# Two-layer hybrid decoder kernel: where the sums of the output weights' quarters are made, the order of the seven products, and which norms fold their halves

## The chip, the cores and the metric

The kernel runs on 1 core of one Trainium2 chip. The metric is device time in microseconds; times are given as the median of 3 runs. A difference of about 0.2% (2.67 us) is what a measurement of this kernel can tell from none.

## The reference, cut to what matters

Two layers act on x of 512 tokens by 1024 channels, float32. Each layer normalises x, multiplies by one wide input matrix, runs differential attention (8 heads) and an mLSTM in chunked form (8 heads), gates both, projects each, merges them to u, and adds an output projection:

```python
for l in range(DEPTH):
    h = rmsnorm(x, norm_g)
    proj = h @ w_in
    ...
    oa = rmsnorm(oa, attn_norm_g) * (1.0 - lam_init)
    ya = (oa * silu(az)) @ w_out_a
    hb = rmsnorm(hb, mlstm_norm_g)
    yb = (sigmoid(bo) * hb * silu(bz)) @ w_out_b
    u = sigmoid(ga) * ya + sigmoid(gb) * yb
    x = x + u @ w_o
```

## The kernel before, in words

Every product is made in three matmuls of high and low parts (`mm3`, L493): an operand a is split into a rounded high part and the rest (`split`, L489: ScalarE copies, VectorE subtracts), and the product takes high times high, high times low and low times high. A weight piece is 128 x 1024 numbers, 512 KB. It is loaded by SyncE into a tile `wr` (tag `raw`, two buffers), split into `wh` and `wl` (three buffers each), and used by TensorE for 24 matmuls of 512 columns, or, for a piece of the output projection, 12.

The output projection `u @ w_o` ("wo") is made in seven half-size products instead of eight (Strassen-Winograd, `seven`, L763). Each product P1 to P7 has two pieces (halves a = 0 and 1) of 12 matmuls. The chains X, Y and Z are accumulators of two banks each (L760): P1, P6, P7 and P4 add up in X, P5 and P3 in Y, P2 in Z. P1, P2 and P3 take quarters of the weights as they are; P5, P6, P7 and P4 take sums of quarters: T1 = first + second quarter, T2 = T1 + a third, T3 = two quarters, T4 = T2 + the last. Before the change these sums are made in SBUF, in tiles `ws_wo` and `wt_wo` out of a pool of 20 slots (`add_up`, L1465): SyncE loads the first quarter into the tile, and a GpSimd DMA that accumulates adds the next. T1 and T3 are made some 12 pieces ahead (`acl`). T2 takes T1's place in the same tile, so its adding transfer can start only when P5's piece has been split out of it, and T4's only after P6's (`prep`, L1505). The order of products is P1 P5 P3 P6 P2 P7 P4, so that P3 covers the time of T2's transfers.

The output's upper right quarter is residual minus X minus Y; in the order before, both are read after P6 (`post`, L767; `wo_out`, L1002).

A sum over the 128 channels of a head, for the norms and the mLSTM's denominator, is a matmul with ones (`psum_over`, L1267). Plain, the squares are split into two tiles and take two matmuls (`hi_lo`, L1262). Folded (`fold`, L1252), the lower 64 partitions' squares get those of the upper 64 added, high and low halves share one tile, and one matmul does; ScalarE makes the square in two instructions of 64 partitions, and VectorE has one more addition. `foldA` lists the attention heads that fold, `foldM` the mLSTM heads for the norm, `foldD` those for the denominator.

The order of work on every engine comes from a planner (`Recorder.schedule`, L272) that records all instructions, gives each a due time worked back from TensorE's order, and takes at each step the ready one with the least due time. Links from a tile's last reader to the next user of its buffer count in the due times (`soft`, L292). SyncE takes what is ready in order of recording. `TUNE` holds the order of the pieces, the due-time margins (`bias` shifts them by tile name) and the offsets of the heads' steps.

Of the kernel before, what the change touches and what calls it, by code (L numbers as in the profile page):

```python
# [18 lines left out]
P = 128  # L19
# [16 lines left out]

TUNE = {
    "order": (
# [4 lines left out]
    ),  # L43
    "qkt": 5,
    "gct": 15,
    "gls": 6,
    "glf": 5,
    "attn": (1, 5, 5, 8, 9, 13, 15, 16, 19, 24),
    "a0": 23,
    "ap": 18,  # L50
    "a4": 7,
    "ml": (1, 9, 11, 12, 13, 28),
    "ahead": 3,
    "lc": 7,
    "slack": 4956.0,
    "margin": 72.0,
    "pemargin": 171.8,
    "wait": 333.1,
    "swpen": 701284048.1,
    "smargin": 51.6,  # L60
    "pwait": 0.8,
    "wdiff": 3673.3,
    "wsp": 4,
    "kact": (0, 2),
    "qsq": (1, 3),
    "foldA": (2, 3, 5),
    "foldM": (0, 1, 2, 3, 4, 7),
    "foldD": (0, 1, 2, 3, 4, 5, 6, 7),
    "warm": 18,
    "start": 'x0 ct ng w0 x1 w1 x2 x3',  # L70
    "prods": 'P1 P5 P3 P6 P2 P7 P4',
    "acl": 12,
    "gateA": 9,
    "gateM": 0,
    "actp": (0, 2, 3),
    "m0": 218,
    "mp": 15,
    "m4": 11,
    "slots": 20,
    "bias": {'av': 27450.0, 'msp_a': -4350.0, 'wl': 2400.0, 'wo': -3700.0, 'woh': -4650.0, 'ht': 29150.0, 'taz': -4050.0, 'ga': 16050.0, 'gt': -8800.0, 'p': -300.0, 'wo1_P': 23900.0, 'out_0_dram': -5900.0, 'p5_wo': -4950.0, 'rot': 12650.0, 'dq': -4400.0, 'oa': 450.0, 'dd': 30900.0, 'num': 20100.0, 'ld': -4700.0, 'ws1_wo': -1200.0, 'gw': -1100.0, 'hl': -350.0, 'sc': -1400.0, 'uz': -3750.0, 'mk': 7250.0, 'sbz': 550.0, 'az': 10300.0, 'posi': -650.0, 'msl_d': 1650.0, 's1_wo': 1700.0, 'wob': 50.0, 'msh_d': 6450.0, 'sq': -1600.0, 'warm': 3150.0, 'bo': -400.0, 'sdl': 200.0, 'ml': 15800.0, 'fo_b': 11200.0, 'ws0_wo': -900.0, 'wt1_wo': 1300.0, 'pb': 2000.0, 'sbo': 5350.0, 'qkt': 2000.0, 'junk': 6150.0, 'ulZ': 7650.0, 'bv': 650.0, 'bqk': -1750.0, 'uh': -3950.0, 'ms_b': -1550.0, 'gi': 1000.0, 'ob': 250.0, 'uy': 1750.0, 'gcol': -750.0, 'ms': 11250.0, 'cosv': -4100.0, 'ms_a': 1450.0, 'ones': 2450.0, 'msh_b': 6650.0, 'x1d': -1650.0, 'qt': 1100.0, 'qk0_2x': -6300.0, 'fb_a': 4650.0, 'saz': 900.0, 'xr': -2300.0, 'fb_b': 900.0, 'wo0_P': 450.0, 'qk1_0x': 1950.0, 'fb_d': -5800.0, 'msh_a': 2700.0, 'ulA': -150.0, 'ang': 150.0, 'rnh': 1400.0, 'gft': 6600.0, 'gct': 200.0, 'gc': -300.0, 'mql': -1200.0, 'rows': 150.0, 'kl': -700.0, 'posf': -150.0, 'zw': 2400.0, 'qk1_2x': -3000.0, 'gf': 450.0, 'qk0_0x': -50.0, 'uhY': 7150.0, 'qs': 3050.0, 'qy': 250.0, 'ul': -500.0, 'msl_a': 2800.0, 'uhZ': 7800.0, 'lneps': -950.0, 'gm': -4350.0, 'lq': 450.0, 'x': -3700.0, 'eps': -700.0, 'sgb': 150.0, 'wr': -400.0, 'wt0_wo': -300.0, 'stab': 8000.0, 'xn': 1200.0, 'qss': 150.0, 'den': 2000.0, 'msl_b': 950.0, 'rn': -150.0, 'glf': 900.0, 'ss': 4250.0, 'bz': -100.0, 'sdh': -200.0, 'em': -250.0, 'uhB': 850.0, 'rq': 250.0, 'sinv': -1650.0},  # L80
    "drain": 251.9,
    "risk": 295.5,
    "late": 912.7,
}


# [358 lines left out]
def kernel(ctx, tc, x, pos, wp, wg, cst, par, pb, ngb, out):  # L445
# [162 lines left out]
    def give(n):  # L608
        state["q2"] -= n
# [16 lines left out]
    def layer_events(l):  # L626
# [136 lines left out]
        def seven(name, lhs, out, over):  # L763
# [63 lines left out]
        def qk_done(c, tt, acc):  # L827
# [38 lines left out]
            st[("rot", tt % 2)] = rq  # L866
            if tt % 2 == 0:
# [592 lines left out]
    def source(l, n, kh, c, a):  # L1460
        return wp[l, KIDX[n, c, 2 * kh + a]]

    chains = {}

    def add_up(l, n, t, a):  # L1465

        if t == "T1":
            take(1)
            chains[n, a] = q2w(f"ws{l}_{n}_{a}", F32)
            SY.dma_start(chains[n, a], source(l, n, 0, 0, a))  # L1470
            G.dma_start(chains[n, a], source(l, n, 0, 1, a), accum_op=ALU.add)
        elif t == "T3":
            take(1)
            chains[n, a, 3] = q2w(f"wt{l}_{n}_{a}", F32)
            SY.dma_start(chains[n, a, 3], source(l, n, 0, 1, a))
            G.dma_start(chains[n, a, 3], source(l, n, 1, 1, a), accum_op=ALU.add)
        else:
            G.dma_start(chains[n, a], source(l, n, 1, 1 if t == "T2" else 0, a), accum_op=ALU.add)

    def load(i):  # L1480
        if i >= len(pieces) or i in loaded:
            return
        l, key = pieces[i]
        if key[0] == "seven":
            _, n, prod, a = key
            if prod in ("P1", "P2", "P3"):
                w = wpool.tile([P, 1024], F32, tag="raw", bufs=2, name=f"wr{i}")
                SY.dma_start(w, source(l, n, *{"P1": (0, 0), "P2": (1, 0), "P3": (1, 1)}[prod], a))
                loaded[i] = w
            return  # L1490
# [7 lines left out]
    def load_sums(i):  # L1498

        if i < len(pieces) and pieces[i][1][0] == "seven" and pieces[i][1][2] in ("P5", "P7") and ("sum", i) not in loaded:  # L1500
            l, (_, n, prod, a) = pieces[i]
            add_up(l, n, {"P5": "T1", "P7": "T3"}[prod], a)
            loaded["sum", i] = True

    def prep(i):  # L1505
        if i >= len(pieces) or i in ready:
# [8 lines left out]
            return  # L1515
        wh = wpool.tile([P, 1024], F32R, tag="wh", name=f"wh{i}")
        wl = wpool.tile([P, 1024], F32R, tag="wl", name=f"wl{i}")
        if key[0] == "seven" and key[2] in ("P5", "P6", "P7", "P4"):
            _, n, prod, a = key
            load_sums(i)  # L1520
            t = chains[n, a, 3] if prod == "P7" else chains[n, a]
            split(wh, wl, t)
            if prod in ("P5", "P6"):
                add_up(l, n, "T2" if prod == "P5" else "T4", a)
            else:
                give(1)
        elif i < TUNE["wsp"]:
            A.copy(wh, loaded[i])
            for hf in range(2):
                cs = slice(S * hf, S * hf + S)  # L1530
                V.tensor_tensor(wl[:, cs], loaded[i][:, cs], wh[:, cs].bitcast(F32), ALU.subtract)
        else:
            split(wh, wl, loaded[i])
# [8 lines left out]
            SY.dma_start(ng0 if n == "ng" else ct, ngb[0] if n == "ng" else cst)  # L1542
    late_loads()
    prep(0)
    for i, run in enumerate(runs):
        if i in starts:
            starts[i](state["t"])
        for a in range(3):
            load(i + a)
        for a in range(TUNE["acl"] + 1):  # L1550
            load_sums(i + a)
        for a in range(TUNE["ahead"]):
            prep(i + a)
        for _ in run(*ready[i]):
# [86 lines left out]
```

## Time and profile before

| | |
|---|---|
| median of 3 runs | 1334.37 us (1334.32 to 1335.81) |
| the profiled execution's own time | 1334.56 us |
| its span, first to last instruction | 1332.5 us |
| TensorE busy | 1325.0 us, 6200 matmuls |
| VectorE busy | 1018.0 us, 1846 instructions |
| ScalarE busy | 907.8 us, 1836 instructions |
| GpSimd busy | 36.9 us, 44 instructions |
| DMA | 148.14 MB, mean 111 GB/s |
| granted TensorE clock | 1.000 |

Busy time is the union of an engine's instructions. Matmuls overlap in the records: one of 512 columns is recorded at some 390 ns, while the next starts earlier, so what a matmul costs is read from a run of them, start to end. `PEld` is the loading of the stationary operand, which overlaps. Lines named `q` (SPq) are a queue's issuing instructions. L441 is the one line from which the planner issues everything, so rows are told apart by tile names.

### The profile page before, as it was taken

Reading aid. Unit: us, or ns where it says so; the run is one execution under the profiler, and the core shown is the slowest. Engines: PE = TensorE matmul, PEld = TensorE weight load, DVE = VectorE, ACT = ScalarE, POOL = GpSimd, SP = SyncE. Lnnn points to the kernel's source line nnn. Section 1 sums busy time; section 2 is a strip of 40 time slices with the busy share of each in tenths; the row PEclk is TensorE's granted clock in tenths of the full one; section 3 lists DMA queues with packets and bytes.
Section 4 is the critical chain, followed back from the end, with each engine's and each line's share of the span. In section 5 each row is a group of like instructions: output and inputs, shape, how many; then the busy total and the mean of one; then the engine's idle time right before and its main releaser. Section 6 shows DMA issues by size and latency. Waiting matters only on the chain.

```text
span 1332.5 us, 17532 instructions
## 1 busy us (share of the span) xinstructions
PE 1325.0 (99%) x6200; PEld 1095.0 (82%) x6200; DVE 1018.0 (76%) x1846; ACT 907.8 (68%) x1836; POOL 36.9 (3%) x44
## 2 busy tenths in 40 slices
PE   9999999999999999999999999999999999999998
PEld 7888888888888888888788888888888888888886
DVE  7898899786259968755888988997852699687566
ACT  6878798877247858743667787889762489687343
POOL 1000000000000000000200000000000000000000
PEclk9999999999999999999999999999999999999999
DMA  5222222223333443554833122222332344354646
GB/s 188 87 67 78 80 83 64 91 79 99 95 103 112 149 123 113 146 155 128 248 112 95 49 95 64 79 76 83 82 112 79 128 119 141 99 135 135 170 122 182
DMA packets 51272, 148.14 MB, mean 111 GB/s; under 512 B 6096, under 2 KB 12880, under 8 KB 51184
## 3 DMA queue, kind: packets, MB, share of 16 engines
q1 hardware_dynamic: 48880, 138.63, 32.9%
q0 software_dynamic: 2304, 8.39, 3.6%
q8 instruction: 49, 0.80, 0.2%
q14 instruction: 39, 0.32, 0.1%
HBM read 142.74 MB, written 4.26 MB: 110 GB/s over the span
## 4 chain that ended last, share of the span: by engine, by line
PE 98%; ACT 1%; DMA 0%; SPq 0%; DVE 0%; issue 0%; DVEq 0%
PE qk L441 13%; PE av L441 9%; PE az L441 7%; PE bv L441 7%; PE bqk L441 7%; PE bz L441 7%; PE bo L441 7%; PE gb L441 7%; PE ga L441 7%; PE woa L441 7%; PE wob L441 7%; PE wo_P L441 6%; PE sc L441 3%; PE num L441 2%; PE ms L441 1%; PE ut L441 1%
## 5 line engine op out<-in xcount | busy, mean ns | idle before, releaser
L441 ACT CAST wh<-wr 128x1024 fp32r<-128x1024 f32 (+1 forms) x206 | 214.8, 1045 | 190.0 <-PE ga L441 36.3
L441 DVE TENSOR_TENSOR wl<-wr,wh 128x1024 fp32r<-128x1024 f32 (+1 forms) x208 | 248.9, 1200 | 99.7 <-ACT wh L441 98.9
L441 PE MATMUL qk<-wh,hh 128*128 128x512 f32 x256 | 96.1, 401 | 0.5 <-ACT hh L441 0.5
L441 PE MATMUL qk<-wh,hl 128*128 128x512 f32 x256 | 95.3, 400 | 0.1
L441 PE MATMUL qk<-wl,hh 128*128 128x512 f32 x256 | 94.8, 396 | 0.5 <-DVE wl L441 0.5
L441 ACT ACTIVATE p<-sc,mx,rq 128x128 f32<-128x128 f32 (+3 forms) x128 | 78.8, 618 | 16.2 <-DVE mx L441 15.6
L441 PE MATMUL woa<-oa,wh 128*128 128x512 f32 x256 | 87.8, 390 | 0.0
L440 ACT ACT_TABLE_LOAD x65 | 83.4, 1283 | 1.1
L441 PE MATMUL wob<-ob,wh 128*128 128x512 f32 x256 | 83.4, 389 | 0.0
L441 PEld LDWEIGHTS qk<-wl,hh 128*128 128x128 f32 x256 | 48.0, 188 | 10.2 <-DVE wl L441 0.9
L441 PEld LDWEIGHTS wob<-ob,wh 128*128 128x128 f32 x256 | 48.1, 188 | 10.1
L441 PEld LDWEIGHTS qk<-wh,hl 128*128 128x128 f32 x256 | 48.0, 188 | 10.0 <-DVE hl L441 0.4
L441 PEld LDWEIGHTS qk<-wh,hh 128*128 128x128 f32 x256 | 47.7, 188 | 10.0 <-ACT hh L441 0.9
L441 PEld LDWEIGHTS woa<-oa,wh 128*128 128x128 f32 x256 | 47.8, 188 | 9.7
L441 DVE TENSOR_REDUCE mx<-sc 128x2 f32<-128x256 f32 (+1 forms) x64 | 52.5, 821 | 1.1
L441 PE MATMUL bqk<-hh,wl 128*128 128x512 f32 x128 | 50.3, 393 | 0.0
L441 PE MATMUL bo<-hh,wl 128*128 128x512 f32 x128 | 50.2, 392 | 0.0
L441 PE MATMUL bo<-hl,wh 128*128 128x512 f32 x128 | 50.1, 391 | 0.0
L441 PE MATMUL bo<-hh,wh 128*128 128x512 f32 x128 | 50.0, 391 | 0.0
L441 PE MATMUL bqk<-hl,wh 128*128 128x512 f32 x128 | 50.0, 393 | 0.0
L441 PE MATMUL az<-hh,wh 128*128 128x512 f32 x128 | 49.8, 397 | 0.0
L441 PE MATMUL gb<-hl,wh 128*128 128x512 f32 x128 | 49.8, 392 | 0.0
(309 smaller groups left out, 3695.9 us busy)
## 6 DMA issues: line engine op xcount, KB each, us to landing
wr<-in_wp_dram SPq DMA_DIRECT2D x204, 512.0 KB, 3.5
ws_wo<-in_wp_dram POOLq DMA_DIRECT2D x12, 512.0 KB, 6.8
dd<-rows SPq DMA_DIRECT2D x16, 256.0 KB, 4.3
em<-rows SPq DMA_DIRECT2D x16, 256.0 KB, 4.0
dd<-rows SPq DMA_DIRECT2D x16, 192.0 KB, 4.8
x<-in_x_dram SPq DMA_DIRECT2D x4, 512.0 KB, 7.4
dd<-rows SPq DMA_DIRECT2D x16, 128.0 KB, 6.0
ws_wo<-in_wp_dram SPq DMA_DIRECT2D x4, 512.0 KB, 5.2
```

The source lines that it names most:

```text
L440: self.tc.keep_in_program_order(self.nc.scalar.preload_act_table_set(self.SET_NAME[o["load"]]))
L441: self.tc.keep_in_program_order(getattr(o["e"], o["fn"])(*o["a"], **o["k"]))
```

## The change

- The sums T1 to T4 become tiles in DRAM. From piece 25 of the first layer and piece 31 of the second, one transfer is issued with each piece, 16 per layer: two plain copies on SyncE and then two adding transfers on GpSimd for each of T1, T3, T2, T4, where T2 begins as a copy of T1 and T4 as a copy of T2. `add_up`, `load_sums` and the SBUF tiles go.
- P5, P6, P7 and P4 load their sums like any other weight piece, through the two `raw` buffers.
- The order of products becomes P1 P5 P6 P3 P2 P7 P4; the upper right quarter is written after P3.
- `foldA` holds all 8 heads instead of 3, `foldM` 8 instead of 6, `foldD` 7 instead of 8.
- The rotary step's two half-width VectorE multiplications become one that reads the halves in reverse order.
- The order of pieces and the planner's numbers differ throughout.

```diff
-    "foldA": (2, 3, 5),
-    "foldM": (0, 1, 2, 3, 4, 7),
-    "foldD": (0, 1, 2, 3, 4, 5, 6, 7),
+    "foldA": (0, 1, 2, 3, 4, 5, 6, 7),
+    "foldM": (0, 1, 2, 3, 4, 5, 6, 7),
+    "foldD": (0, 1, 2, 3, 4, 5, 6),
-    "prods": 'P1 P5 P3 P6 P2 P7 P4',
-    "acl": 12,
+    "prods": 'P1 P5 P6 P3 P2 P7 P4',
+    "sums0": 25,
+    "sums1": 31,
...
-                elif prod == "P6":
+                elif prod == max("P3", "P6", key=seq.index):
                     out(0, 1, t, Y[t], X[t])
...
-            for hf in range(2):
-                o = 32 * hf
-                V.tensor_tensor(
-                    s4[:, :, :, o : o + 32],
-                    a4[:, :, :, 32 - o : 64 - o],
-                    stab[:, tt, :, o : o + 32].unsqueeze(2).to_broadcast([P, 2, 4, 32]),
-                    ALU.mult,
-                )
+            a5, s5_ = (x.rearrange("p (i g h d) -> p i g h d", i=2, g=4, h=2) for x in (acc, r2))
+            stb = stab[:, tt].rearrange("p i (h d) -> p i h d", h=2).unsqueeze(2).to_broadcast([P, 2, 4, 2, 32])
+            V.tensor_tensor(s5_, a5[:, :, :, ::-1, :], stb, ALU.mult)
...
+    def sum_steps(l, n):
+        t = {(p, a): dram.tile([P, D + 16], F32, name=f"{p}{l}_{n}_{a}")[:, :D] for p in ("T1", "T2", "T3", "T4") for a in range(2)}
+        for p, q in (("P5", "T1"), ("P6", "T2"), ("P7", "T3"), ("P4", "T4")):
+            for a in range(2):
+                sums[l, n, p, a] = t[q, a]
+        for first, then in ((("T1", (0, 0)), ("T1", (0, 1))), (("T3", (0, 1)), ("T3", (1, 1))), (("T2", "T1"), ("T2", (1, 1))), (("T4", "T2"), ("T4", (1, 0)))):
+            for step, (d, b) in enumerate((first, then)):
+                for a in range(2):
+                    yield lambda d=d, b=b, a=a, e=G if step else SY, k={"accum_op": ALU.add} if step else {}: e.dma_start(t[d, a], t[b, a] if isinstance(b, str) else source(l, n, *b, a), **k)
...
-        if key[0] == "seven" and key[2] in ("P5", "P6", "P7", "P4"):
-            _, n, prod, a = key
-            load_sums(i)
-            t = chains[n, a, 3] if prod == "P7" else chains[n, a]
-            split(wh, wl, t)
-            if prod in ("P5", "P6"):
-                add_up(l, n, "T2" if prod == "P5" else "T4", a)
-            else:
-                give(1)
-        elif i < TUNE["wsp"]:
+        if i < TUNE["wsp"]:
...
+        elif key[0] == "seven":
+            _, n, prod, a = key
+            SY.dma_start(w, source(l, n, *{"P1": (0, 0), "P2": (1, 0), "P3": (1, 1)}[prod], a) if prod in ("P1", "P2", "P3") else sums[l, n, prod, a])
...
+        l = pieces[i][0]
+        if i - l * len(layers[0][0]) >= TUNE["sums1" if l else "sums0"]:
+            for f in [next(todo[l], None)]:
+                if f:
+                    f()
+
+                    rec.ops[-1]["pre"].setdefault(state["load"], 0)
```

More of the change, by code (lines that the diff above doesn't have):

```diff
@@ L50 @@
     "ap": 18,
-    "a4": 7,
-    "ml": (1, 9, 11, 12, 13, 28),
+    "a4": 10,
+    "ml": (3, 11, 12, 12, 13, 28),
     "ahead": 3,
-    "lc": 7,
+    "lc": 11,
     "slack": 4956.0,
-    "margin": 72.0,
-    "pemargin": 171.8,
+    "margin": 86.0,
+    "pemargin": 94.9,
     "wait": 333.1,
-    "swpen": 701284048.1,
-    "smargin": 51.6,
-    "pwait": 0.8,
+    "swpen": 13796308115.6,
+    "smargin": 39.8,
+    "pwait": 0.4,
     "wdiff": 3673.3,
-    "wsp": 4,
+    "wsp": 3,
     "kact": (0, 2),
@@ L77 @@
     "mp": 15,
-    "m4": 11,
+    "m4": 26,
     "slots": 20,
-    "bias": {'av': 27450.0, 'msp_a': -4350.0, 'wl': 2400.0, 'wo': -3700.0, 'woh': -4650.0, 'ht': 29150.0, 'taz': -4050.0, 'ga': 16050.0, 'gt': -8800.0, 'p': -300.0, 'wo1_P': 23900.0, 'out_0_dram': -5900.0, 'p5_wo': -4950.0, 'rot': 12650.0, 'dq': -4400.0, 'oa': 450.0, 'dd': 30900.0, 'num': 20100.0, 'ld': -4700.0, 'ws1_wo': -1200.0, 'gw': -1100.0, 'hl': -350.0, 'sc': -1400.0, 'uz': -3750.0, 'mk': 7250.0, 'sbz': 550.0, 'az': 10300.0, 'posi': -650.0, 'msl_d': 1650.0, 's1_wo': 1700.0, 'wob': 50.0, 'msh_d': 6450.0, 'sq': -1600.0, 'warm': 3150.0, 'bo': -400.0, 'sdl': 200.0, 'ml': 15800.0, 'fo_b': 11200.0, 'ws0_wo': -900.0, 'wt1_wo': 1300.0, 'pb': 2000.0, 'sbo': 5350.0, 'qkt': 2000.0, 'junk': 6150.0, 'ulZ': 7650.0, 'bv': 650.0, 'bqk': -1750.0, 'uh': -3950.0, 'ms_b': -1550.0, 'gi': 1000.0, 'ob': 250.0, 'uy': 1750.0, 'gcol': -750.0, 'ms': 11250.0, 'cosv': -4100.0, 'ms_a': 1450.0, 'ones': 2450.0, 'msh_b': 6650.0, 'x1d': -1650.0, 'qt': 1100.0, 'qk0_2x': -6300.0, 'fb_a': 4650.0, 'saz': 900.0, 'xr': -2300.0, 'fb_b': 900.0, 'wo0_P': 450.0, 'qk1_0x': 1950.0, 'fb_d': -5800.0, 'msh_a': 2700.0, 'ulA': -150.0, 'ang': 150.0, 'rnh': 1400.0, 'gft': 6600.0, 'gct': 200.0, 'gc': -300.0, 'mql': -1200.0, 'rows': 150.0, 'kl': -700.0, 'posf': -150.0, 'zw': 2400.0, 'qk1_2x': -3000.0, 'gf': 450.0, 'qk0_0x': -50.0, 'uhY': 7150.0, 'qs': 3050.0, 'qy': 250.0, 'ul': -500.0, 'msl_a': 2800.0, 'uhZ': 7800.0, 'lneps': -950.0, 'gm': -4350.0, 'lq': 450.0, 'x': -3700.0, 'eps': -700.0, 'sgb': 150.0, 'wr': -400.0, 'wt0_wo': -300.0, 'stab': 8000.0, 'xn': 1200.0, 'qss': 150.0, 'den': 2000.0, 'msl_b': 950.0, 'rn': -150.0, 'glf': 900.0, 'ss': 4250.0, 'bz': -100.0, 'sdh': -200.0, 'em': -250.0, 'uhB': 850.0, 'rq': 250.0, 'sinv': -1650.0},
@@ L81 @@
-    "drain": 251.9,
-    "risk": 295.5,
-    "late": 912.7,
+    "bias": {'av': 30550.0, 'msp_a': -4700.0, 'wl': 1050.0, 'wo': -3700.0, 'woh': -4650.0, 'ht': 32950.0, 'gt': -8100.0, 'ld': -19300.0, 'sc': -1750.0, 'qkt': 8500.0, 'ulZ': 9950.0, 'bv': 2950.0, 'bqk': -1850.0, 'ob': -5650.0, 'msh_b': 6650.0, 'msh_a': 2700.0, 'kl': -550.0, 'msl_a': 2800.0, 'msl_b': 950.0, 'ulY': 4000.0, 'bz': -3450.0, 'gb': -1750.0, 'stab': -14200.0, 'ms_a': -3750.0, 'dd': -4750.0, 'ws0_wo': -1300.0, 'ws1_wo': 150.0, 'wob': -1050.0, 'glf': -8400.0, 'wt1_wo': 6400.0, 'oa': -1050.0, 'wt0_wo': 100.0, 'T10_wo': 4150.0, 'saz': -2100.0, 'ut': 1300.0, 'ct': -2000.0, 'az': -1900.0, 'xr': -4150.0, 'qy': 5750.0, 'wh': 8400.0, 'num': 3100.0, 'den': 9000.0, 'T41_wo': -3650.0, 'wo0_P': -400.0, 'rot': -900.0, 'fb_b': -3700.0, 'mk': 5450.0, 'ks': 2100.0, 'qk0_0x': 1250.0, 'qk1_0x': -400.0, 'rows': -1100.0, 'T20_wo': -6950.0, 'posi': 650.0, 'ctab': 3900.0, 'mql': -1000.0, 'uh': -1700.0, 'hl': -200.0, 's1_wo': 1300.0, 'sums': 4200.0, 'ul': -900.0, 'x': -10200.0, 'ss': -3550.0, 'ulA': -4700.0, 'T31_wo': 2750.0, 'wo1_P': 400.0, 'ms_b': -6650.0, 'ulB': 6750.0, 'qk': 700.0, 'lneps': -950.0, 'gc': 4050.0, 'tbz': -350.0, 'T30_wo': -1650.0, 'ng': -100.0, 'lq': -450.0, 'wr': -1500.0, 'sgb': 550.0, 'posf': 2250.0, 'qk0_2x': 3900.0, 'T40_wo': 3650.0, 'junk': -1700.0, 'fb_d': -2150.0, 'ms': 650.0, 'gf': -550.0, 'T21_wo': -1750.0, 'mq': 2600.0, 'gft': 2950.0, 'rnh': 7150.0, 'qt': -400.0, 'hh': -400.0, 'gct': 2100.0, 'qk1_2x': -350.0, 'T11_wo': -2400.0, 'sinv': -3700.0, 'ang': -750.0, 'dq': -1550.0, 'eps': 6050.0, 'mx': 900.0, 'epsc': -1600.0, 'sbz': 1400.0, 'uy': 4600.0, 'taz': 1200.0, 'uhB': -100.0, 'pb': -500.0, 'msp_b': 8450.0, 'cv': 350.0, 'zw': -4650.0, 'xn': 400.0, 'uhZ': 200.0, 'qss': -3450.0, 'sdh': -950.0, 'rn': 200.0, 'zeroc': 7250.0, 'ones': 4950.0, 'p5_wo': 100.0, 'fo_b': -2550.0, 'gm': 750.0, 'ua': 1550.0, 'qs': 150.0, 'fo_a': 50.0, 'gi': -300.0, 'gw': -1000.0},
@@ L84 @@
+    "drain": 239.1,
+    "risk": 233.4,
+    "late": 751.9,
 }
@@ L1461, in source @@
         return wp[l, KIDX[n, c, 2 * kh + a]]
[L1463 to L1476, printed above, removed]
-        else:
-            G.dma_start(chains[n, a], source(l, n, 1, 1 if t == "T2" else 0, a), accum_op=ALU.add)
+    sums = {}
+    def sum_steps(l, n):
[7 more added lines that the diff above has]
+                    yield lambda d=d, b=b, a=a, e=G if step else SY, k={"accum_op": ALU.add} if step else {}: e.dma_start(t[d, a], t[b, a] if isinstance(b, str) else source(l, n, *b, a), **k)
     def load(i):
@@ L1496, in load @@
         loaded[i] = w
[L1498 to L1503, printed above, removed]
+        state["load"] = len(rec.ops) - 1
     def prep(i):
@@ L1544 @@
     prep(0)
+    todo = [sum_steps(l, "wo") for l in range(depth)]
     for i, run in enumerate(runs):
```

24 lines of the change are left out of this document (7 added, 17 removed), and 8 rows, old and new, of the table TUNE.

## The prediction, made before the result was known

> **What bounds the kernel now.** I read the page first, then the chain that ended last, then TensorE's waits.
>
> ```profile
> span 1332.5 us, 17532 instructions
> PE 1325.0 (99%) x6200; PEld 1095.0 (82%) x6200; DVE 1018.0 (76%) x1846; ACT 907.8 (68%) x1836; POOL 36.9 (3%) x44
> PE 98%; ACT 1%; DMA 0%; SPq 0%; DVE 0%; issue 0%; DVEq 0%
> ```
>
> TensorE is busy for 1325.0 of 1332.5 us and holds 98% of the chain. What it waits for in the whole run is short:
>
> ```profile
> PE warm L441 <- DVE ml L441: 1.6, 1, 1.6
> PE qk L441 <- ACT hh L441: 0.5, 1, 0.5
> PE ht L441 <- DVE junk L441: 0.5, 2, 0.3
> PE qk L441 <- DVE wl L441: 0.5, 1, 0.5
> PE wo_P L441 <- ACT p_wo L441: 0.3, 1, 0.3
> PE wo_P L441 <- ACT wh L441: 0.3, 1, 0.3
> ```
>
> The sum is 3.7 us, of which 3.1 us fall in the first microseconds (warm-up, first norm, first pieces) and 0.6 us in the output projection. So only two things can move the time by much: the number of matmuls, and new waits of TensorE. The price of a matmul is read from an undisturbed run of them in the chain:
>
> ```profile
> 468.08 14.74 PE bv L441 x65
> ```
>
> 14.74 us for 65 is 0.2268 us for one of 512 columns.
>
> **The folds.** These rows are the matmuls over a low half that a plain head needs and a folded one does not:
>
> ```profile
> L441 PE MATMUL msp_a<-msl_a,ones 128*128 128x512 f32 x10 | 3.9, 394 | 0.0
> L441 PE MATMUL msp_b<-msl_b,ones 128*128 128x512 f32 x4 | 1.6, 393 | 0.0
> ```
>
> All 10 + 4 go, as both lists become full. One head's denominator unfolds in each of two layers, which adds 2. Net 12 fewer, 12 x 0.2268 = 2.72 us, on the path because TensorE is the path. In return a head that folds has more work off the path:
>
> ```profile
> L441 ACT ACTIVATE ms_a<-av 128x512 f32<-128x512 f32 x10 | 5.9, 590 | 2.0 <-PE av L441 2.0
> L441 ACT ACTIVATE fb_a<-av 64x512 f32<-64x512 f32 x6 | 3.6, 596 | 0.1
> L441 DVE TENSOR_TENSOR ms_a<-ms_a,fb_a 64x512 f32<-64x512 f32 x6 | 4.1, 683 | 1.0 <-ACT fb_a L441 0.9
> 25.00:350.00 325.00, 325.00 (x1565) 268.27 (x1564) 271.13 (x590) 253.90 (x635) 4.75 (x5) 1.00 0.26 83
> ```
>
> The columns of the last row are TensorE, weight loads, VectorE, ScalarE and GpSimd busy, then clock, DMA share and GB/s. A square of 64 partitions takes as long as one of 128 (0.596 against 0.590 us), so a fold costs ScalarE 0.60 and VectorE 0.68 us; 12 net cost 7.2 and 8.2 us over the run. The attention's part, five heads in a layer, is 3.0 and 3.4 us in a stretch of 325 us in which the two are idle for 71 and 54 us. I cost it at nothing on the path; if that cover were gone, a head's norm would come 1.3 us later, and who waits is one matmul of that head, with weight pieces to run in between.
>
> **The rotary step.**
>
> ```profile
> L441 DVE TENSOR_TENSOR sq<-qk,stab 128x256 f32<-128x256 f32 x64 | 25.5, 416 | 0.3
> L441 DVE TENSOR_TENSOR rot<-qk,ctab 128x512 f32<-128x512 f32 x32 | 21.9, 684 | 0.2
> ```
>
> Two instructions of 0.416 us become one of the size of the second row, 0.684 us: 0.15 us, 32 times, 4.7 us off VectorE in all, which pays for over half of the folds. The reversed read is not in the trace; between 0.684 and twice that VectorE ends 5 us lighter to 17 us heavier, and I take the equal size. Nothing on the path.
>
> **The sums, made ahead.** Per layer, 8 plain and 8 adding transfers now run beside pieces 25 to 40 (31 to 46 in the second layer), and 8 loads of sums are new; on SyncE that is 12 issues more, on GpSimd as many as before. Room for them:
>
> ```profile
> q1 hardware_dynamic: 48880, 138.63, 32.9%
> q0 software_dynamic: 2304, 8.39, 3.6%
> 160.00:310.00 150.00, 150.00 (x731) 123.71 (x730) 130.14 (x280) 126.08 (x319) 1.90 (x2) 1.00 0.26 79
> ```
>
> 32.9% of the span for 138.63 MB is 1.66 us for 512 KB; 3.6% for 8.39 MB in 16 adding transfers is 3.0 us each. A transfer from DRAM to DRAM is not in the trace; between once and twice these prices, 16 of them hold the DMA for 37 to 75 us, next to the 39 us (0.26 of 150) used in the stretch where they land. They fit. They would matter only by holding SyncE, which issues the weights too:
>
> ```profile
> ws_wo<-in_wp_dram POOLq DMA_DIRECT2D x12, 512.0 KB, 6.8
> L441 PE MATMUL bv<-wh,hh x128: 387/389/485, 268.0 to 1150.8; 128*128 128x512 f32 x128
> SPq L441 <- DVE wl L441: 998.2, 189, 14.6
> ```
>
> The first bv piece is number 38 and starts at 268 us, so pieces are some 7 us apart there. T4's copy is issued two pieces, 14 us, behind the adding transfer that it needs, and that lands in 6.8 us. If it came late, the weight loads queued behind would first use up SyncE's own idle time (998.2 / 189 = 5.3 us per load) and then the two pieces split ahead, 14 us. GpSimd's zeroing of the kl and mql tiles queues behind the adds; 8 issues are few there. Cost: nothing.
>
> **The output projection.** Two terms. First, with the sums ready, P6 follows P5 while P5's result is copied out of Y; the wait for p_wo (0.3 us) goes. The other 0.3 us was for P2's weights, late because their load ran beside adding transfers:
>
> ```profile
> q0 software_dynamic: 548, 1.98, 59.6%
> wr<-in_wp_dram SPq DMA_DIRECT2D x4, 512.0 KB, 7.5
> wr<-in_wp_dram SPq DMA_DIRECT2D x22, 512.0 KB, 3.5
> ```
>
> The first two rows are the DMA view of 638 to 656 us, the last that of 160 to 310 us: beside adding transfers, which alone hold 59.6% of the engines, a weight load lands in 7.5 us, without them in 3.5. The Trainium skill ("DMA: Bandwidth & Descriptors", Queues, rings and completion order) has each DMA engine take turns between queues packet by packet; the trace agrees (7.5 against 3.5 us), so the adds taken away should give back what they took. Gain of both waits: 0.6 us.
>
> Second, the price: all 14 pieces now pass the two raw buffers, 8 of them for the first time, and a piece lasts only 12 x 0.2268 = 2.72 us here. One turn of a buffer is read off here:
>
> ```profile
> 652.25 1.05 ACT L441 CAST wh<-wr 128x1024 fp32r<-128x1024 f32 x1 [2.14 <-DMA wr<-in_wp_dram]
> 653.33 1.23 DVE L441 TENSOR_TENSOR wl<-wr,wh 128x1024 fp32r<-128x1024 f32 x1 [0.64 <-ACT wh L441]
> 654.59 0.33 SPq L441 DMA_DIRECT2D wr<-in_wp_dram  x1
> ```
>
> Copy 1.05, subtraction 1.23, each followed by 0.03 to the next step, the load 3.5, and 0.03 more: 5.87 us, for two buffers 2.93 us a piece. That is slower than TensorE's 2.72. It lives on what is ready when the stage begins:
>
> ```profile
> 630.53 0.39 PE L441 MATMUL wo_P<-wh,uhA 128*128 128x512 f32 x1
> 630.55 1.05 ACT L441 CAST wh<-ws_wo 128x1024 fp32r<-128x1024 f32 x1 [2.12 <-PE wob L441]
> 633.74 1.22 DVE L441 TENSOR_TENSOR wl<-ws_wo,wh 128x1024 fp32r<-128x1024 f32 x1
> ```
>
> P5's first half is copied as P1 begins; its subtraction, which will free the buffer for P6, could end at 630.55 + 1.05 + 0.03 + 1.23 = 632.86, 2.33 us after P1's start, but in this trace it ended at 634.96, 4.43 after, behind VectorE's work on u. Five turns later comes P4's first half: 2.33 + 5 x 5.87 = 31.7 us, due at 12 x 2.72 + 0.23 = 32.9. So with a prompt subtraction there is 1.2 us to spare, with one as late as here a wait of 0.9 us in each layer. I take the prompt one: before, nothing hung on that tile's release, while now the planner's links through the raw buffers pull the subtraction's due time forward. For the load, the ends are 3.5 us (quiet) and 7.5 us (beside adds), and 3.5 is nearer, since no adds are left in the stage. Cost: 0 as likeliest. By the Trainium skill's figure (same page, Anatomy of one DMA) of 2.0 us plus bytes at 436 GB/s, the load would be an estimated 3.2 us, and the spare time 2.7 us; the measured 3.5 is used.
>
> **The sum.** -2.72 - 0.6 = -3.3 us. The profiled execution took 1334.56 us (1332.5 span and 2.1 around it), 0.2 above the median of 1334.37; it would come out at 1331.2, and the median at 1331.0 us.
>
> **Rivals.** *The raw buffers starve TensorE (slower).* Each microsecond on the load's landing adds five turns' worth by the end: the wait per layer is 5 x (landing - 3.5) - 1.2. For a busy stage speaks:
>
> ```profile
> xr<-in_x_dram SPq DMA_DIRECT2D x8, 256.0 KB, 4.5
> ```
>
> The residual's loads, half the size, land in 4.5 us in this very stage, and they stay. At 4.5 us for the weights the wait is 3.8 us a layer, 7.6 in all, and the time 1331.0 + 7.6 = 1338.6. It undoes the gain from a landing of 4.06 us on (1.65 us a layer) and shows as slower from 4.35. Against it: part of the 4.5 was itself queueing beside adding transfers. The Trainium skill ("HBM Reference", Latency) has an access go from 0.2 to 2 us under high load; by it the landing would be an estimated 5.3 us and the time near 1347; the trace shows no high load without adding transfers, so this bears only on the chance.
>
> *The subtraction stays late (no change).* VectorE is full at the start of the stage as now, 0.9 us lost in each layer: 1331.0 + 1.8 = 1332.8. A landing of 3.8 to 4.3 us with a prompt subtraction ends in the same place.
>
> *The sums in DRAM hold SyncE (slower).* The Trainium skill ("DMA: Bandwidth & Descriptors", Anatomy of one DMA) warns that a DMA's completion can take surprisingly long when the target is HBM. From rows: to reach TensorE an adding transfer must outlast 14 + 5 + 14 = 33 us; at 40 us, six times the 6.8 above, 7 us a layer are lost, 1345 us. Against it:
>
> ```profile
> x1d<-xn SPq DMA_DIRECT2D x8, 256.0 KB, 2.0
> ```
>
> Stores to DRAM land in 2.0 us here.
>
> **How the numbers follow.** About 0.2%, 2.67 us, can be told from no change: faster means under 1331.7, slower over 1337.0. The forecast has 0.53, late subtraction or a mild queue 0.25, starved buffers 0.17, SyncE held 0.05. That gives faster 0.53, same 0.25, slower 0.22. The range goes down by the 3.1 us of waits at the start, which another order of work may shorten, to 1327.9, and up to 1338.6. The forecast's own range is 1327.9 to 1331.7.
>
> **What would show it.** Right: 6188 matmuls; no msl_a or msl_b rows; no wait of TensorE for p_wo; no adding transfer in the output projection; weight loads landing there in 3.5 to 3.8 us; P5's first subtraction within 3 us of P1's start. Wrong: TensorE waiting for wh or wl of P2, P7 or P4 by a microsecond or more, with loads landing above 4 us; waits of SyncE for T1 or T2 over 5 us; or TensorE waits for msp tiles in the attention stretch, which would mean that the folds' cover is gone.

## The result and the profile after

| | before | after |
|---|---|---|
| median of 5 runs, same chip | 1334.97 us | 1341.94 us (1340.05 to 1343.85) |
| ratio | | 1.0055, 95% interval 1.0043 to 1.0066 |
| profiled execution, its span | 1334.56, 1332.5 us | 1343.85, 1341.7 us |
| TensorE | 1325.0 us, 6200 matmuls | 1326.2 us, 6188 matmuls |

The change costs 7 us, where 3.3 us were expected back, and the time lies above the range. TensorE has its 12 matmuls fewer, and is busy longer all the same. The page of the kernel after, its span, busy times and chain:

```profile
span 1341.7 us, 17554 instructions
PE 1326.2 (99%) x6188; PEld 1091.6 (81%) x6188; DVE 1027.4 (77%) x1825; ACT 911.1 (68%) x1844; POOL 36.2 (3%) x44
PE 92%; DVE 3%; DMA 3%; ACT 1%; issue 0%; SPq 0%; DVEq 0%; ACTq 0%
```

TensorE held 98% of the chain before. Now 92%, with transfers and VectorE in its place. TensorE's waits in the kernel after:

```profile
PE wo_P L442 <- ACT wh L442: 3.1, 3, 1.4
PE wo_P L442 <- DVE wl L442: 2.7, 4, 0.9
PE ht L442 <- DVE junk L442: 2.1, 3, 1.3
PE warm L442 <- DVE ml L442: 1.6, 1, 1.6
PE qk L442 <- ACT wh L442: 0.7, 1, 0.7
PE den L442 <- DVE fo_d L442: 0.6, 1, 0.6
PE qk L442 <- DVE wl L442: 0.4, 2, 0.2
PE wo_P L442 <- DVE xn L442: 0.2, 1, 0.2
```

They come to 11.4 us against 3.7. The wait for p_wo is gone, and 5.8 us of waits for the high and low parts of the output projection's weights are new. Where the time went is read from stretches cut at the starts of the first and the last matmul into wo_P, so that the first and third are the main work of a layer and the second and fourth its output projection. Columns: length, TensorE busy, weight loads, VectorE, ScalarE, GpSimd, clock, DMA share, GB/s. The kernel before, then the kernel after:

```profile
0.00:630.53 630.53, 627.31 (x2941) 518.69 (x2942) 481.10 (x900) 437.67 (x898) 15.18 (x20) 1.00 0.34 107
630.53:670.97 40.44, 40.10 (x181) 32.10 (x179) 34.47 (x48) 24.78 (x36) 7.25 (x8) 1.00 0.81 237
670.97:1289.81 618.84, 618.84 (x2914) 513.12 (x2913) 471.52 (x858) 427.87 (x881) 11.05 (x12) 1.00 0.34 102
1289.81:1328.53 38.72, 38.41 (x169) 31.09 (x167) 30.16 (x41) 17.49 (x22) 3.45 (x4) 1.00 0.69 190
```

```profile
0.00:630.10 630.10, 626.38 (x2935) 517.53 (x2935) 486.11 (x891) 439.50 (x902) 18.25 (x24) 1.00 0.39 114
630.10:677.36 47.26, 42.54 (x186) 32.31 (x184) 35.76 (x53) 25.21 (x37) 3.80 (x4) 1.00 0.69 232
677.36:1295.57 618.21, 617.53 (x2904) 510.83 (x2902) 475.36 (x844) 428.75 (x884) 14.11 (x16) 1.00 0.37 110
1295.57:1337.67 42.10, 39.33 (x169) 30.94 (x167) 29.24 (x39) 17.65 (x22) 0.00 (x0) 1.00 0.64 219
```

The two main stretches are 0.4 and 0.6 us shorter. The whole loss lies in the output projections: 47.26 for 40.44 and 42.10 for 38.72, 6.8 and 3.4 us. Together that is the 9.2 us between the two spans (the profiled execution after is 1.9 us above its median, hence more than the 7.0 of the medians). The DMA view of the first one, 635 to 672 us, in the kernel after:

```profile
q1 hardware_dynamic: 3365, 8.74, 69.9%
...
wr<-T_wo SPq DMA_DIRECT2D x5, 512.0 KB, 4.8
wr<-in_wp_dram SPq DMA_DIRECT2D x5, 512.0 KB, 4.9
x1d<-xn SPq DMA_DIRECT2D x5, 256.0 KB, 4.6
xr<-in_x_dram SPq DMA_DIRECT2D x4, 256.0 KB, 5.4
ng<-in_ngb_dram SPq DMA_DIRECT2D x1, 512.0 KB, 7.0
```

No adding transfer is left, yet a weight load lands in 4.8 to 4.9 us, not 3.5 (medians of the few landings that the trace has in this window; single loads of the projection took 3.3 to 6.3 us): residual loads, stores of the new x and the next layer's constants go through the same queue. One bad moment in SyncE's timeline of the kernel after, and then TensorE and ScalarE at the end of it (idle time and its releaser in brackets):

```profile
652.92 0.33 SPq L442 DMA_DIRECT2D wr<-T_wo  x1
653.35 0.37 SPq L442 DMA_DIRECT2D ng<-in_ngb_dram  x1
654.30 0.33 SPq L442 DMA_DIRECT2D x1d<-xn  x1
654.68 0.42 SPq L442 DMA_DIRECT2D xr<-in_x_dram  x1
655.20 1.30 SPq L442 DMA_DIRECT2D x1d<-xn  x1
```

```profile
658.51 0.39 PE L442 MATMUL wo_P<-wl,uhB 128*128 128x512 f32 x1
...
659.19 1.04 ACT L442 CAST wh<-wr 128x1024 fp32r<-128x1024 f32 x1 [2.79 <-DMA wr<-T_wo]
...
660.28 0.50 PE L442 MATMUL wo_P<-wh,uhZ 128*128 128x512 f32 x1 [1.38 <-ACT wh L442]
660.62 0.39 PE L442 MATMUL wo_P<-wh,ulB 128*128 128x512 f32 x1
```

The load issued at 652.92 shares its time with four transfers behind it; its copy starts at 659.19, 6.3 us later. TensorE is idle for 1.38 us by the record, but from start to start it takes 660.28 - 658.51 = 1.77 instead of 0.227, and the next step 0.34. So one such wait costs 1.54 + 0.11 = 1.65 us, 0.27 more than its idle time, since the matmuls around it stand further apart. Four waits at that price make 1.1 us, about as much as TensorE is busy longer in the second projection (39.33 against 38.41 us), which has four. In the first, 42.54 against 40.10 us, there are five waits, and five more matmuls fall into the stretch (186 for 181), four of them the next layer's; what is left of the 2.4 us was not followed up.

### The profile page after: what moved, and what is told of

Read it like the earlier page. It is cut to its first block, busy times and chain, and to the rows that moved or that the text cites. A ratio compares the mean times of both kernels' runs of the same rounds, so it can differ in the third digit from the quotient of the medians.

```text
span 1341.7 us, 17554 instructions
## 1 busy us (share of the span) xinstructions
PE 1326.2 (99%) x6188; PEld 1091.6 (81%) x6188; DVE 1027.4 (77%) x1825; ACT 911.1 (68%) x1844; POOL 36.2 (3%) x44
## 4 chain that ended last, share of the span: by engine, by line
PE 92%; DVE 3%; DMA 3%; ACT 1%; issue 0%; SPq 0%; DVEq 0%; ACTq 0%
PE qk L442 13%; PE av L442 9%; PE az L442 7%; PE woa L442 7%; PE bv L442 7%; PE ga L442 7%; PE bo L442 7%; PE bqk L442 7%; PE wob L442 6%; PE gb L442 6%; PE bz L442 5%; PE sc L442 3%; PE wo_P L442 2%; PE num L442 2%; DVE wl L442 1%; PE ut L442 1%
## 5 line engine op out<-in xcount | busy, mean ns | idle before, releaser
L442 ACT CAST wh<-wr 128x1024 fp32r<-128x1024 f32 (+1 forms) x222 | 231.3, 1045 | 187.2 <-PE wob L442 32.7
L442 DVE TENSOR_TENSOR wl<-wr,wh 128x1024 fp32r<-128x1024 f32 (+1 forms) x223 | 268.6, 1206 | 102.3 <-ACT wh L442 99.8
L442 PE MATMUL qk<-wh,hh 128*128 128x512 f32 x256 | 99.4, 401 | 0.7 <-ACT wh L442 0.7
L442 PE MATMUL qk<-wh,hl 128*128 128x512 f32 x256 | 98.4, 399 | 0.0
L442 PE MATMUL az<-hh,wl 128*128 128x512 f32 x128 | 50.3, 398 | 0.0
L442 PE MATMUL bqk<-hh,wh 128*128 128x512 f32 x128 | 50.3, 393 | 0.0
```

The costliest lines, as they stand in the source:

```text
L442: self.tc.keep_in_program_order(getattr(o["e"], o["fn"])(*o["a"], **o["k"]))
```

## The experiments

All were timed in 5 rounds beside the kernel before, whose median in these rounds was 1334.5 to 1335.2 us; differences are of medians. Except for the doubled matmuls, the planner wrote the order of work anew for each kernel, so each of these runs changes the order too. The theory at the start was that the ring of two raw buffers cannot feed TensorE in this stage. Its rivals: the sums in DRAM, the residual's loads, the order of products, the folds.

**The sums in DRAM left out.**

```diff
-... else sums[l, n, prod, a])
+... else source(l, n, 0, 1, a))
-    todo = [sum_steps(l, "wo") for l in range(depth)]
+    todo = [iter(()) for l in range(depth)]
```

> The changed kernel with the sums left out altogether: no transfers between pieces 25 and 46, and P5, P6, P7 and P4 load a plain quarter of the weights through the same two raw buffers (so the output projection is computed with wrong weights). Ring theory (two raw buffers turn too slowly for pieces of 2.72 us while other transfers lengthen the landing): still 1340 to 1343 us, output projection 46 to 48 us in the first layer and 41 to 43 in the second. Sums theory (adding into DRAM, or reading sums from it, is what costs): 1331 to 1334 us, output projections near 40.5 and 38.7 us.

1342.53 us, ratio 1.0057 (1.0043 to 1.0071); projections 45.8 and 42.1 us, with 2.2 and 2.7 us of waits for wh and wl. The loss stays without a single adding transfer: making the sums is not its cause.

**No residual loads.**

```diff
-            SY.dma_start(xr, xres[tt * P : (tt + 1) * P, c * S : (c + 1) * S])
+            G.memset(xr, 0.0)
```

> The changed kernel with the residual's 16 loads left out: GpSimd writes zeros in their place (so the residual is not added). Ring theory: the weight loads in the output projection land in 3.5 to 4.2 us instead of 4.8, and the waits for wh and wl there fall from 5.8 us to under 2.5; 1335 to 1338 us. Rival, that the ring is too slow even with quiet loads, or that the subtractions are late: landing falls, waits stay above 4 us, 1339 to 1342 us.

1338.10 us, 1.0022 (1.0013 to 1.0032); projections 44.3 and 40.6 us, with 1.5 us of waits for wh and wl left and 1.7 for xr. Without the residual's loads 3.8 us come back, but it is still 3.6 us above the kernel before. Not all of the 3.8 can be put down to quicker loads: by the medians the weights landed in 3.4 to 3.8 us in the second projection, but still in 4.5 to 4.6 in the first.

**Four pieces taken out of the ring.** The sums stay in DRAM; those of P7 and P4 are loaded into the free SBUF slots, 18 pieces ahead.

```diff
+        if key[0] == "seven" and key[2] in ("P7", "P4"):
+            return
...
+    held = {}
+    def hold(i):
+        if i < len(pieces) and i not in held and pieces[i][1][0] == "seven" and pieces[i][1][2] in ("P7", "P4"):
+            l, (_, n, prod, a) = pieces[i]
+            take(1)
+            held[i] = q2w(f"wt{l}_{n}_{prod}{a}", F32)
+            SY.dma_start(held[i], sums[l, n, prod, a])
...
+        if i in held:
+            split(wh, wl, held[i])
+            give(1)
...
+        for a in range(18):
+            hold(i + a)
```

> The changed kernel, but the sums for P7 and P4 are loaded from DRAM into four of the 20 SBUF slots ahead (the slots the SBUF sums held before the change), so only 10 of the 14 pieces pass the raw buffers. Ring theory: output projections near 41 and 39 us, 1332 to 1335 us, under the kernel before. Rival, that the planner's numbers or the order of products cost the time: 1339 to 1342 us.

1334.30 us, 1.0001 (0.9993 to 1.001): 7.6 us below the kernel after. The waits in the projections fall from 5.8 to 1.5 us:

```profile
PE wo_P L442 <- DVE wl L442: 0.9, 2, 0.6
...
PE wo_P L442 <- ACT wh L442: 0.6, 1, 0.6
```

So taking four pieces out of the ring gives the loss back, as the ring theory expected. Two of its numbers were missed: the first projection takes 43.0 us, not 41, and the time is level with the kernel before, not under it.

**The ring put into the kernel before.** With before's folds, order and numbers, the sums are made in DRAM and all 14 pieces pass through the ring; `add_up` and `load_sums` go.

```diff
-        if key[0] == "seven" and key[2] in ("P5", "P6", "P7", "P4"):
-            _, n, prod, a = key
-            load_sums(i)
...
-        elif i < TUNE["wsp"]:
+        if i < TUNE["wsp"]:
...
+        elif key[0] == "seven":
+            _, n, prod, a = key
+            SY.dma_start(w, source(...) if prod in ("P1", "P2", "P3") else sums[l, n, prod, a])
```

> The kernel before with one part of the change alone: the sums made in DRAM ahead (pieces 25 and 31 on) and loaded through the raw buffers; folds, order of products and all the planner's numbers as before. Ring theory: the output projections grow by about 7 and 3 us as in the changed kernel, 1341 to 1347 us, and the main stretches by at most 2 us. Rival, that the changed kernel's other numbers made its output projections slow: projections within 2 us of 40.4 and 38.7, 1335 to 1337 us.

1350.85 us, 1.0118 (1.0102 to 1.0133); projections 49.1 and 43.4 us, 8.6 and 4.7 more than before, main stretches 1.4 and 1.2 more. The time is above the 1341 to 1347 that were expected. The ring costs here too, with the old folds, order and numbers. In the second projection the landings that the trace has are 3.4 to 4.0 us, so it costs even where these loads are quick; in the first they are 3.4 to 6.6. SyncE, VectorE and TensorE in the second projection of this kernel:

```profile
1319.06 2.79 SPq L441 DMA_DIRECT2D wr<-in_wp_dram  x2
...
1323.73 1.23 DVE L441 TENSOR_TENSOR wl<-wr,wh 128x1024 fp32r<-128x1024 f32 x1 [2.24 <-ACT wh L441]
1324.88 2.47 DVE L441 TENSOR_TENSOR xr<-xr,wo_P 128x512 f32<-128x512 f32 x4
...
1324.99 0.33 SPq L441 DMA_DIRECT2D wr<-T_wo  x1
...
1326.90 0.47 PE L441 MATMUL wo_P<-wh,uhB 128*128 128x512 f32 x1 [2.53 <-DVE xr L441]
```

One buffer's turn is 1324.99 - 1319.06 = 5.93 us, against 2 x 2.72 = 5.44 that TensorE needs. The late subtraction also holds the four reads of accumulators behind it on VectorE, and TensorE waits 2.53 us for those: the same lateness under the name xr.

**The unused sums added to the kernel before**, with its own SBUF sums kept:

```diff
+    todo = [sum_steps(l, "wo") for l in range(depth)]
...
+        if i - l * len(layers[0][0]) >= (31 if l else 25):
+            for f in [next(todo[l], None)]:
+                if f:
+                    f()
```

> The kernel before, and beside it the 32 transfers that make the sums in DRAM, with the result not used. If making the sums ahead costs nothing on the path: 1334 to 1336 us, as before. If they hold SyncE or slow the weight loads: 1338 us or more, with TensorE waiting for wh or wl between pieces 25 and 46.

1335.85 us, 1.0009 (1.0000 to 1.0018): 32 transfers more in the run cost 0.9 us by the medians, and 2.4 at the upper end of the interval. They are not what costs 7.

**The old order of products.**

```diff
-    "prods": 'P1 P5 P6 P3 P2 P7 P4',
+    "prods": 'P1 P5 P3 P6 P2 P7 P4',
```

> The changed kernel with the order of products of before, P1 P5 P3 P6 P2 P7 P4. Ring theory: all 14 pieces still pass the raw buffers, so nothing is won, 1340.5 to 1343.5 us. Rival, that P6 right behind P5 is what brings the waits (its operands of u are made late): 1335 to 1338 us.

1342.35 us, 1.0056 (1.0044 to 1.0069): no difference from after (1341.94). The order of products is not the cause. Its projections take 46.9 and 41.2 us, and TensorE waits there for xr and xn (4.0 us) more than for wh and wl (1.8).

**The old folds in the kernel after, and the new ones in the kernel before.**

```diff
-    "foldA": (0, 1, 2, 3, 4, 5, 6, 7),
-    "foldM": (0, 1, 2, 3, 4, 5, 6, 7),
-    "foldD": (0, 1, 2, 3, 4, 5, 6),
+    "foldA": (2, 3, 5),
+    "foldM": (0, 1, 2, 3, 4, 7),
+    "foldD": (0, 1, 2, 3, 4, 5, 6, 7),
```

> The changed kernel with the fold lists of before: 12 matmuls more, less work on ScalarE and VectorE. If the folds' matmuls lie on the path and their cost does not, 2.7 us slower than the changed kernel: 1344 to 1345 us. If the folds' extra work delays others (the den wait of 0.6 us, the busier attention stretch): 1340 to 1342 us.

1350.86 us, 1.0119 (1.0105 to 1.0133): 8.9 us above after, three times the 2.7.

> The kernel before with only the fold lists of the changed kernel: 12 matmuls fewer. If a fold's price in the main stretches is 12 x 0.2268 us and its work on ScalarE and VectorE hides there under any plan: 2.7 us faster than before, 1331.5 to 1332.5 us. Rival, after the undoing of the folds cost 8.9 us where 2.7 were expected: the plan's numbers fit one set of folds, and any change of it costs waits of TensorE in the attention stretch; then 1335 to 1341 us, with waits for wl or dd.

1352.32 us, 1.0129 (1.0115 to 1.0143): slower too. Both miss, because the planner writes another order for a changed list and meets waits all over the main stretches (638.8 and 629.1 us in the second kernel, 630.5 and 618.8 before). TensorE's waits in that kernel:

```profile
PE wob L441 <- ACT ob L441: 2.9, 2, 1.4
PE ut L441 <- DVE mx L441: 2.4, 1, 2.4
PE wob L441 <- DVE ob L441: 1.7, 2, 0.8
```

The granted clock falls there as well, to 0.50 from 813 to 819 us. So neither run prices a fold; each prices a plan whose numbers were made for other folds.

**The folded norms' matmuls issued twice**, in the kernel after. The planner does not see the second, so its order stays.

```diff
+            if o["kind"] in ("msp_a", "msp_b"):
+                self.tc.keep_in_program_order(getattr(o["e"], o["fn"])(*o["a"], **o["k"]))
```

> The changed kernel with its plan untouched: when the planned instructions are issued, each of the 32 ones-matmuls of the heads' norms is issued twice, the second overwriting the first (same result). It prices a matmul of the folds without a new plan. If such matmuls lie on the path at 0.2268 us: 32 x 0.2268 = 7.3 us more than the changed kernel, 1348 to 1350.5 us. Rival, that TensorE has slack there behind ScalarE and VectorE: under 3.5 us more, 1342 to 1345.5 us.

1349.19 us, 1.0104 (1.0088 to 1.0119): 7.25 us above after for 32 matmuls, 0.227 each. The main stretches, 16 such matmuls in each, grew from 630.1 to 633.8 and from 618.2 to 622.2 us, by 3.7 and 4.0 where 16 x 0.2268 is 3.6. So a norm's matmul lies on the path at the price that the prediction used, where the order is kept. (The profiled execution, 1354.49 us, is 5.3 us above the median: it has 3.8 us more in the second projection as well, where a wait of 2.1 us was followed by a lower clock.)

**Other sets of pieces out of the ring.** All eight sums, through four slots (P7's and P4's loads follow P5's and P6's splits):

```diff
+            follow = {"P5": "P7", "P6": "P4"}.get(key[2])
+            if follow:
+                hold(pieces.index((l, ("seven", "wo", follow, key[3]))), (follow,))
...
+        for a in range(12):
+            hold(i + a)
```

> The changed kernel, but all eight sums are loaded from DRAM into four of the 20 SBUF slots: P5's and P6's halves 12 pieces ahead, and P7's and P4's into the same slots as soon as those are split; only P1, P3 and P2 pass the raw buffers, as before the change. Ring theory: no wait for wh or wl over 0.5 us in the output projections, 40.5 and 38.5 us long, and with the folds' 2.7 us 1330.5 to 1333 us, under the kernel before. Rival, that the loads' contention and not the number of raw turns is what costs: no better than with half of the sums held, 1334 to 1336 us.

1337.49 us, 1.0019 (1.001 to 1.0028): a miss. The waits for wh and wl in the projections are gone, but one of 2.0 us for xn in the first and one of 1.0 us for xr in the second take their place, and the clock falls after the longer (last section).

The sums of P6 and P7 alone, 14 ahead:

```diff
+        if key[0] == "seven" and key[2] in ("P6", "P7"):
+            return
...
+        for a in range(14):
+            hold(i + a)
```

> The changed kernel, with the sums for P6 and P7 (not P7 and P4) loaded ahead into four of the SBUF slots, so that the pieces that pass the raw buffers come in runs of four, four and two with held pieces between, in place of one run of ten. If the ring lives on the lead it has at the start of a run, as in the prediction's reckoning: less wait for wh and wl than with P7 and P4 held (1.5 us), output projections at most 42 and 38.8 us, 1331.5 to 1334 us, faster than the kernel before. Rival, that what is left is the residual's loads, late in the same queue: waits for xr or xn in place of those for wh and wl, 1334 to 1337 us.

1335.09 us, 1.0005 (0.9996 to 1.0014): the rival's time and the rival's wait. The second projection takes 37.85 us and has no wait left; the first takes 43.45, with one wait of 2.3 us for xn, since VectorE there does first a subtraction whose load is late, then xn. (The profiled execution, 1337.16 us, is 2.1 above the median.)

**The planner told of slower transfers.** The order of work is written for loads at 360 B/ns. In e9's kernel the price is lowered to 260:

> The kernel with the sums of P6 and P7 held, and the planner's price of a load from DRAM raised from 512 KB at 360 bytes per ns plus 2.0 us (3.46 us) to 260 bytes per ns (4.0 us), nearer to what loads take in the output projection. If the wait of 2.3 us for xn there came of an order written for loads that land too early: no wait for xn over 0.5 us, first output projection 42 us or less, 1331.5 to 1334 us. Rival, that a new plan brings waits elsewhere, as the changes of folds did: 1336 to 1345 us.

1338.12 us, 1.0024 (1.0015 to 1.0034). The projections fall to 40.0 and 37.9 us, but the main stretches, planned anew, rise to 631.8 and 622.3 with new waits (qk for wl 2.1, sc for p 1.0, ga for ua 0.8). So next the price was lowered for the output projection's loads alone:

```diff
+        dst = o["a"][0].tensor.name
+        if dst[:2] == "wr" and int(dst[2:].split("_")[0]) % 111 > 96 or dst[:2] in ("xr", "wt"):
+            return 260.0
```

> The kernel after, with the sums of P6 and P7 held in four of the SBUF slots 14 pieces ahead (as in e9_hold_p6_p7), and with the planner's price for a transfer lowered from 360 to 260 B/ns for the output projection's weight and residual loads alone, so that the order there is written for loads that land about a microsecond later while the rest keeps its price. If what was left in e9 was an order written for loads too early, the output projections come out at 40.0 and 37.9 us as in e12_hold_slow_price, the main stretches at 629.6 and 617.1 us as in e9 and e3, and the time is 1328 to 1332 us, below both kernels. If the order of work is fragile as a whole, the other stages pay some us and it stays at 1334 to 1338 us.

1333.75 us, 0.9989 (0.998 to 0.9997): 8.2 us below after, and 1.5 below before, which is less than the 0.2% that a measurement can tell: level with the kernel before. Its output projections, and the weights' loads in the first of them:

```profile
631.24:671.09 39.85, 39.65 (x177) 32.12 (x176) 32.85 (x46) 24.70 (x36) 3.80 (x4) 1.00 0.70 232
...
1291.00:1328.85 37.85, 37.85 (x168) 31.23 (x167) 29.10 (x39) 17.71 (x22) 0.00 (x0) 1.00 0.56 190
```

```profile
wr<-in_wp_dram SPq DMA_DIRECT2D x6, 512.0 KB, 3.9
xr<-in_x_dram SPq DMA_DIRECT2D x8, 256.0 KB, 4.6
...
wr<-T_wo SPq DMA_DIRECT2D x2, 512.0 KB, 4.7
```

The DMA share is as in the kernel after (0.70, 0.69) and the loads are little faster, but ten pieces pass the ring instead of 14, and TensorE has 0.2 us idle in the two projections together (7.5 after). The main stretches, 631.2 and 619.9 us, missed the 629.6 and 617.1 that were expected, and so did the time its 1328 to 1332. Those two numbers are e3's; e9's own stretches were 630.0 and 620.1 us, so beside e9 only the first rose.

The lower price alone, the ring as in the kernel after:

> The kernel after with that lower price for the output projection's loads alone; all 14 pieces still pass the two raw buffers. If the two-buffer ring itself is what costs, it stays at 1338 to 1343 us with TensorE waiting for wh and wl. If the order written for early loads is what costs, it falls to 1331 to 1335 us.

1348.93 us, 1.0098 (1.0083 to 1.0114): worse by 7.0 us and above both expectations, projections 51.5 and 43.7, the first with a fall of the clock (last section). An order written for late loads does not help while 14 pieces pass two buffers. The same price in e3's kernel:

> e3_slots (sums of P7 and P4 held in four slots) with that lower price for the output projection's loads alone. If the waits left in e3 (0.9 us for wl, 0.6 for wh, 43.0 us in the first output projection) come from an order written for early loads, the first output projection falls to about 40 us and the time to 1330 to 1332 us. If not, it stays at 1333 to 1336 us.

1339.30 us, 1.0029 (1.0017 to 1.004), 5.0 us above e3: a miss; projections 44.1 and 41.4 us. The price helps with P6 and P7 held and hurts with P7 and P4 held. It is no remedy by itself, and why the two differ was not followed up. Side by side, the runs say more for the ring than any one of them: taking P7 and P4 out of it gives back 7.6 us at the old price (e3 against after) and 9.6 at the lower one (e15 against e14).

## Why the prediction was wrong

**The step that failed** is the second term of the output projection: "Cost: 0 as likeliest", from a landing of 3.5 us, "since no adds are left in the stage". The landing there is 4.8 to 4.9 us by the medians, 6.3 at the worst, and the two projections grew by 10.2 us. The adding transfers had not been the only neighbours: the row of the residual's loads (4.5 us before) was read as an effect of the adds, and it is 5.4 without them. That row stood in the prediction as the rival's evidence and should have set the value. With no adds in DRAM at all the loss stays (e1), so what the weights wait behind is the stage's own plain traffic; e2, without the residual's part of it, gives 3.8 us back.

**The rival named it.** "The raw buffers starve TensorE" has the wait of a layer as 5 x (landing - 3.5) - 1.2. At 4.85 that is 5.6 us for the first projection. In the second, six loads land in 4.7 and four in 3.5 us, on average 4.2, which gives 2.4. Together 8.0 us. TensorE's idle time grew by 4.72 - 0.34 = 4.4 and 2.77 - 0.31 = 2.5, 6.9 in all; its busy time by 2.4 and 0.9, 3.3 in all, in part from the restarts after waits. These make the 10.2 us. That 8.0 comes near 6.9 is in part luck, since the landings behind it are few and the turns held more than late loads. (1.3 us of the idle time is for junk, the next layer's norm, which starts within the first projection's stretch and was late with it.) The rival's mechanism is shown by e3 (7.6 us back when four pieces leave the ring) and by e10 (13.3 us of projections lost when it is put into the kernel before); its price lacked the restarts, and 4.5 us was still too quick.

**The turns themselves.** The trace has each step of the ring, so the prediction's reckoning of it can be redone with measured times. It had P5's first subtraction end at 2.33 us, five turns of 5.87 us, and P4's first half split at 31.7, due at 32.9. Measured, in us from P1's start:

| | P5's first subtraction ends | five turns | P4's first half split | late by | projection longer than before |
|---|---|---|---|---|---|
| after, first | 2.5 | 37.8 | 40.3 | 7.4 | 6.8 |
| after, second | 2.8 | 34.1 | 36.9 | 4.0 | 3.4 |
| e10, first | 5.4 | 34.8 | 40.2 | 7.3 | 8.6 |
| e10, second | 5.4 | 31.9 | 37.3 | 4.4 | 4.7 |

The subtraction of P4's first half in the first projection of the kernel after (P1 starts at 630.10), and that of P5's first half in e10 (P1 starts at 631.89):

```profile
669.15 1.22 DVE L442 TENSOR_TENSOR wl<-wr,wh 128x1024 fp32r<-128x1024 f32 x1
```

```profile
636.10 1.22 DVE L441 TENSOR_TENSOR wl<-wr,wh 128x1024 fp32r<-128x1024 f32 x1
```

What a projection loses agrees to within 1.3 us with how late P4's first half is, so the way of reckoning was right and its sizes were wrong. In the first projection of the kernel after, the first four turns took 28.9 us instead of 23.5. Their loads took 3.7, 5.5, 3.7 and, from issue to copy, 6.3 us, and that is about 5 of the 5.4 us more: the landing was the term of the sum that was mis-sized. The fifth turn took 8.9 us; the landing of its load is not in the trace, and its copy and subtraction also came behind the next layer's norm on ScalarE and the next layer's rotary tables on VectorE. In e10 the first subtraction came 3.1 us behind the 2.33, after VectorE's work on u: there the rival of the late subtraction came true beside the starved ring. How much of e10's loss comes of its plan, whose numbers were not made for the ring, is open.

**Right.** The prompt subtraction: P1 starts at 630.10, and P5's first subtraction ends 2.5 us later (2.33 predicted).

```profile
631.38 1.23 DVE L442 TENSOR_TENSOR wl<-wr,wh 128x1024 fp32r<-128x1024 f32 x1
```

The sums ahead at no cost that the runs can tell: SyncE has no wait for T1 or T2 in the kernel after, and e6 bounds the cost at 2.4 us. The adding transfers land in 5.7 us, the copies from DRAM to DRAM in 5.6. The folds' 0.2268 us a matmul (e11) and their cover: in 25 to 350 us TensorE is busy for 324.98 of 325.00 us, and no norm's tile is waited for there. In the main stretches of the kernel after TensorE is busy 626.38 + 617.53 = 1243.9 us against 1246.2, 2.2 less of the 2.7 predicted; idle time there grew from 3.2 to 4.4 us (the first pieces, and 0.6 for the denominators' fo_d, one place where a fold is waited for), which leaves the 1.0 us. The rotary step:

```profile
L442 DVE TENSOR_TENSOR sq<-qk,stab 128x512 f32<-128x512 f32 x32 | 21.8, 680 | 0.1
```

The reversed read costs nothing extra (680 ns; the product beside it took 684).

**The forecast's own sum.** e13 is the change without its starved ring, and gains 1.5 us by the medians, less than can be told from none, where the sum had 3.3. Its profiled execution (1334.64 us, 0.9 above its median) has TensorE busy for 1323.7 us, 1.3 less than before, and 4.5 + 0.8 = 5.3 us idle in the main stretches, 2.1 more than before. So a part of the gain was there, and waits of the new plan in the main stretches take the rest; which of its steps set them was not settled.

## What to carry to other kernels

When work is moved to a ring of buffers, compare the ring's turn with the consumer's time at the landing that transfers of the same queue show in that very stage, not in a quiet one; here the turn was reckoned 8% over the consumer's time with quick loads, and the ring became the bound. Keep some pieces out of the ring before looking at the price of anything else. And where a planner writes the order, changing one list replans everything: price a part by a run that leaves the order alone, such as issuing a matmul twice.

## What the runs showed of the hardware

A wait of TensorE can cost more than itself: in some runs the granted clock fell after one. In e9, after the wait of 2.29 us that ended at 654.42, the clock column stands at 0.59 for four microseconds:

```profile
655.00:659.00 4.00, 4.00 (x13) 3.10 (x12) 1.00 (x1) 0.00 (x0) 0.00 (x0) 0.59 0.92 268
659.00:663.00 4.00, 4.00 (x19) 3.31 (x18) 1.82 (x2) 1.62 (x2) 0.00 (x0) 0.98 0.58 222
```

13 matmuls run there instead of 17 or 18. The same followed waits of 2.0 us in e7 (0.71 and 0.72 in two stretches of 3 us) and 3.4 us in e14 (0.50). In the kernel after, whose longest wait in the projections is 1.4 us, the clock column stays at 1.00. But in e10 the wait of 2.53 us left it at 1.00 as well, while in the same run two short waits in a row, 1.32 us ended at 10.16 and 0.46 ended at 12.20, were followed by 0.51 (12 to 15 us). So the length of one wait does not decide alone; what else does was not tried.
